# Layer 1's third pair of down weights placed behind x's rooms, and four norm steps beside each first product of the MLA

## Chip, cores and metric

One core of a Trainium2 chip runs the whole kernel in one launch. The metric is the device time of that launch in microseconds (us). Five engines work side by side, each through its own queue in order: TensorE (PE, matmuls; PEld is its loading of stationary operands), VectorE (DVE), ScalarE (ACT), GpSimd (POOL) and SyncE (SP), which here only issues transfers (DMA).

## The reference

Two layers over 1024 latent tokens (`lat`) and 256 context tokens (`cx`) of width 1024, all in float32. Layer 0 mixes with a gated MLP and a gated DeltaNet, layer 1 with multi-head latent attention (MLA); each layer ends in a convolutional feed-forward network (FFN), and a final norm follows. Cut to what matters here:

```
def conv_ffn(h, w_up, conv_w, w_down):
    g, u = jnp.split(dwconv(h @ w_up, conv_w), 2, axis=-1)      # 2 x 2816 columns
    return (jax.nn.silu(g) * u) @ w_down
...
def mla_mixer(h_ctx, h_lat, w_in, ...):
    z_lat = h_lat @ w_in          # 384 query, 256 key/value, 64 rotary columns
    ...
for i in range(2):
    h_lat = modulate(rms_norm(lat, norm1_g[i]), sh1, sc1)       # the same for the context
    lat = lat + g1 * mixer(h_lat)
    lat = lat + g2 * conv_ffn(modulate(rms_norm(lat, norm2_g[i]), sh2, sc2), w_up, conv_w, w_down)
return rms_norm(lat, final_g)
```

## The kernel before

Activations lie transposed: 128 features on the partitions, tokens along the row. Every float32 product is made of three matmuls on halves: an operand is split into a high half (`...h`, rounded) and a low half (`...l`, the rest), and hh, hl and lh are summed in PSUM. A weight tile of 128x1024 is loaded by a DMA (`wdr`, `wur`: raw), its high half is made on POOL (line 126) and its low half on DVE (line 133).

The instructions are recorded in the order of the Python code, where generators advance side work in steps; a scheduler then sets the final order of each engine's queue from a timeline that it simulates when the kernel is built, under the dependences between tiles. On the chip each engine keeps that order.

**FFN.** `ffn_up` makes the 22 gated rows (`y1`) one after the other: products into PSUM, copies into `raw0` and `raw1`, the convolution into `y0` and `y1`, the gate (line 427) and a store to DRAM (`act<-y`, line 428). These four rows of 4 KB a partition lie in the pool `ffc1` (layer 1). `ffn_down` then takes chunks of tokens (in layer 0 512, 256, 256, 256; in layer 1 512, 256, 256). A chunk has two halves of four output tiles, a half has 11 steps, a step is one weight tile and 24 matmuls (lines 633 to 635, output `dn`). The activations come back from DRAM in groups (`al<-act`, line 571; split into `ah` on ACT and `al` on DVE). The first two weight tiles are prepared inside `ffn_up`'s last round. Which room a pair of halves gets is told by its number i:

```
p, bufs = (wp, 2) if i % 3 < 2 else (self.ffz, 1)
W[i] = [p.tile([P, KD, P], F32R, tag="wu" + a, name="wd" + a, bufs=bufs) for a in "hl"]
```

So pairs 2, 5, 8, ... use the pool `ffz1`. I call the pairs of layer 1's down product W0, W1, W2, ...: W0 is `wdh_26813`, W1 `wdh_26857`, W2 `wdh_26889` (from `wdr_26861`), W3 `wdh_26928`, W4 `wdh_26965`, W5 `wdh_26995`, W6 `wdh_27032`, W7 `wdh_27062`. The pool `ffx1` holds the residual chunks (`x`), which are loaded from DRAM and to which a half's products are added (line 650) at its end. Pools are allocated one behind the other: `ffz1` was allocated first, at the address where `ffc1` lay (bytes 85568 to 93760 of a partition, which were `raw0` and `raw1` of the up stage), then `ffx1` (93760 to 118336).

**The norm at the end of layer 0.** When a chunk of layer 0's down product is done, `tail0` norms and modulates it into `h` for layer 1 (`mod_h`): squares on ACT and POOL, four matmuls of 32 rows each for two sums (`nsum`, line 196), a copy on DVE (line 214), one matmul (`nall`, line 217), a chain over DVE and ACT (lines 219 to 230), then the modulated halves `h1h`, `h1l`, `h2h`, `h2l`. With `steps` it is a generator of ten steps. For the last chunk (256 tokens, `x_15250`) four of them run beside the down product, and `self.pend` holds the other six: four with squares (the first of these four issues the first `nsum`), one with the second `nsum` and its copy, and one with `nall` and all the rest. `mla_early` makes the MLA's first products (`proj`, lines 140 to 142): two weight tiles t for three chunks c of 512, 256 and 256 tokens. `mla_in` then makes those two products for the last chunk, which need its `h`, and goes on with norms of keys (`nsum<-nsq`) and the queries' products.

Of the kernel before, what the change touches and what calls it, by code (L numbers as in the profile page):

```python
# [61 lines left out]
def drain(*gens):  # L62
    for g in gens:
        for _ in g:
            pass
# [32 lines left out]
class Kern:  # L98
# [445 lines left out]
    def ffn_down(self, l, wp, chunks, groups, tile_x, x, g2, tail, early=None):  # L544
# [59 lines left out]
        def run():  # L604
# [49 lines left out]
            self.pend = pend  # L654
        self.X = X
        return run()

    def tail_rooms(self, pool):
# [835 lines left out]
    def mla_early(self, get, hv, pend):  # L1494

        ps = {}
        for t in range(KVT):
            for c in range(3):
                ps[t, c] = self.proj(get(t), hv, None, *CHB[c])
                next(pend, None)  # L1500
            get(t + 1)
        drain(pend)
        return ps
# [328 lines left out]
    def run(self):  # L1832
        nc, tc, I = self.nc, self.tc, self.I
        with ExitStack() as es:
# [208 lines left out]
            xp = []  # L2043
# [75 lines left out]
            def tail1(i):  # L2119
# [4 lines left out]
                for k in range(KD):  # L2124
# [7 lines left out]
                    if k % 2:  # L2132
# [4 lines left out]
            down = self.ffn_down(1, ffw, END, groups, None, load_x(END), lambda c0: g2[:, 0], tail1)  # L2137
            self.ffn_up(1, ffw, SEQ, (0, lambda t: t.rearrange("p (s c) -> p s c", c=256)[:, 2:4, :]), [(0, SEQ, 0)], None,
                        (begin0, begin1, begin2), late, down)
            self.ffz = tc.alloc_tile_pool(name="ffz1", bufs=1)  # L2140
            xp.append(tc.alloc_tile_pool(name="ffx1", bufs=1))
            tp = tc.alloc_tile_pool(name="fft1", bufs=1)
            tmp1 = self.tail_rooms(tp)
            drain(down)
            drain(self.pend)
            tp.release()
            xp[0].release()
            self.ffz.release()
            hcl.release()
            hce.release()  # L2150
            ffw.release()
# [82 lines left out]
```

## Time and profile before

| | |
|---|---|
| median of 3 runs | 3269.45 us (3264.09 to 3271.99) |
| the profiled execution | 3260.52 us, of which the span from first to last instruction 3258.5 us |
| PE busy | 3104.7 us, 95% of the span |
| DVE, POOL, ACT busy | 2165.1, 1306.6, 1103.8 us |
| PE's longest wait | 13.16 us, at 2982 to 2995 us of the span |

Times in rows are microseconds from the start of the span, durations of groups are means in ns. A row of a timeline has start, duration, engine, line, operation, output and inputs, shapes and count, and in brackets how long the engine had idled before and what released it. The releaser is inferred from semaphores. Matmuls overlap: one of 256 columns is shown with 0.28 us, but the next starts 0.12 us later, so rates are read from starts.

### The profile page before, as it was taken

Reading aid. Unit: us, or ns where it says so; the run is one execution under the profiler, and the core shown is the slowest. Engines: PE = TensorE matmul, PEld = TensorE weight load, DVE = VectorE, ACT = ScalarE, POOL = GpSimd, SP = SyncE. Lnnn points to the kernel's source line nnn. Section 1 sums busy time; section 2 is a strip of 40 time slices with the busy share of each in tenths; the row PEclk is TensorE's granted clock in tenths of the full one; section 3 lists DMA queues with packets and bytes.
Section 4 is the critical chain, followed back from the end, with each engine's and each line's share of the span. In section 5 each row is a group of like instructions: output and inputs, shape, how many; then the busy total and the mean of one; then the engine's idle time right before and its main releaser. Section 6 shows DMA issues by size and latency. Waiting matters only on the chain. (4 is left out here: it accounts for less than half of the span.)

```text
span 3258.5 us, 48694 instructions
## 1 busy us (share of the span) xinstructions
PE 3104.7 (95%) x19029; PEld 2596.4 (80%) x19029; DVE 2165.1 (66%) x3218; ACT 1103.8 (34%) x2136; POOL 1306.6 (40%) x1181
## 2 busy tenths in 40 slices
PE   7999899998999999999999999999999899998998
PEld 5667777896777788888899778988978787776888
DVE  6333877566876578874577456666667888887365
ACT  5322233333432233340111255555533333333110
POOL 4234323553443354532455132122134566663243
PEclk9999999999999999999999999999999999999999
DMA  7344957753144522145467131000033122225464
GB/s 253 123 143 126 302 142 217 223 168 117 40 147 147 160 96 70 64 154 173 143 225 223 54 115 38 27 22 22 8 121 119 51 79 81 82 82 207 141 196 150
DMA packets 254436, 411.40 MB, mean 126 GB/s; under 512 B 46576, under 2 KB 163520, under 8 KB 254080
## 3 DMA queue, kind: packets, MB, share of 16 engines
q1 hardware_dynamic: 254208, 408.31, 39.1%
q8 instruction: 150, 2.46, 0.3%
q14 instruction: 78, 0.64, 0.1%
HBM read 327.47 MB, written 80.78 MB: 125 GB/s over the span
## 5 line engine op out<-in xcount | busy, mean ns | idle before, releaser
L633 PE MATMUL dn<-ah,wdh 128*128 128x256 f32 (+1 forms) x1232 | 388.9, 317 | 15.8 <-POOL wdh L126 13.7
L635 PE MATMUL dn<-ah,wdl 128*128 128x256 f32 (+1 forms) x1232 | 383.8, 318 | 14.5 <-DVE wdl L133 14.5
L634 PE MATMUL dn<-al,wdh 128*128 128x256 f32 (+1 forms) x1232 | 386.7, 315 | 0.0
L126 POOL TENSOR_SCALAR wdh<-wdr 128x1024 fp32r<-128x1024 f32 x154 | 194.5, 1264 | 361.6 <-PE dn L634 232.5
L133 DVE TENSOR_TENSOR wdl<-wdr,wdh 128x1024 fp32r<-128x1024 f32 x154 | 200.2, 1304 | 198.1 <-POOL wdh L126 194.2
L633 PEld LDWEIGHTS dn<-ah,wdh 128*128 128x128 f32 x1232 | 235.4, 191 | 38.1 <-POOL wdh L126 14.7
L635 PEld LDWEIGHTS dn<-ah,wdl 128*128 128x128 f32 x1232 | 233.1, 191 | 33.8 <-DVE wdl L133 17.3
L634 PEld LDWEIGHTS dn<-al,wdh 128*128 128x128 f32 x1232 | 235.2, 191 | 15.3
L126 POOL TENSOR_SCALAR wuh<-wur 128x1024 fp32r<-128x1024 f32 x106 | 138.8, 1310 | 215.6 <-PE upc L409 112.1
L133 DVE TENSOR_TENSOR wul<-wur,wuh 128x1024 fp32r<-128x1024 f32 x106 | 164.2, 1549 | 90.9 <-POOL wuh L126 90.9
L1720 POOL TENSOR_SCALAR p<-p,rsm 128x1280 f32<-128x1280 f32 x63 | 84.6, 1343 | 325.9 <-DVE rsm L1713 176.9
L675 DVE SCALAR_TENSOR_TENSOR y<-raw,fconv,y 128x1023 f32<-128x1023 f32 (+1 forms) x132 | 175.0, 1354 | 31.8 <-ACT y L420 31.4
L140 PE MATMUL proj<-hh,wih 128*128 128x512 f32 (+1 forms) x512 | 183.9, 361 | 0.0
L677 DVE SCALAR_TENSOR_TENSOR y<-raw,fconv,y 128x1023 f32<-128x1023 f32 (+1 forms) x132 | 182.9, 1407 | 0.1
L142 PE MATMUL proj<-hh,wil 128*128 128x512 f32 (+1 forms) x512 | 177.2, 347 | 1.1 <-DVE wil L133 1.1
L141 PE MATMUL proj<-hl,wih 128*128 128x512 f32 (+1 forms) x512 | 177.7, 348 | 0.0
L427 POOL TENSOR_TENSOR y<-y,y 128x1280 f32<-128x1280 f32 (+1 forms) x42 | 119.8, 2852 | 108.1 <-issue 58.0
L393 POOL TENSOR_TENSOR s<-wur 128x512 f32<-128x512 f32 x42 | 70.2, 1671 | 183.2 <-DMA wur<-in_w_up 142.2
L1702 DVE TENSOR_REDUCE mx<-sc 128x1 f32<-128x512 f32 (+1 forms) x192 | 114.5, 596 | 40.2 <-PE sc L1701 38.1
L420 ACT ACTIVATE y<-raw,fconv 128x1280 f32<-128x1280 f32 (+1 forms) x88 | 110.6, 1259 | 81.1 <-DVE raw L436 74.7
L111 ACT ACTIVATE p<-sc,nmx 128x512 f32<-128x512 f32 (+1 forms) x192 | 116.0, 617 | 49.3 <-DVE nmx L1706 49.1
L140 PEld LDWEIGHTS proj<-hh,wih 128*128 128x128 f32 x512 | 98.3, 193 | 20.2 <-issue 7.7
(544 smaller groups left out, 9290.3 us busy)
## 6 DMA issues: line engine op xcount, KB each, us to landing
wdr<-in_w_down SPq DMA_DIRECT2D x154, 512.0 KB, 3.8
adaw<-in_ada_w SPq DMA_DIRECT2D x96, 512.0 KB, 4.2
wur<-in_w_up SPq DMA_DIRECT2D x88, 512.0 KB, 3.6
al<-act SPq DMA_DIRECT2D x20, 1024.0 KB, 7.7
t<-t SPq DMA_DIRECT2D x20, 768.0 KB, 6.4
act<-y SPq DMA_DIRECT2D x22, 640.0 KB, 2.9
act<-y SPq DMA_DIRECT2D x22, 512.0 KB, 2.6
wir<-in_w_t SPq DMA_DIRECT2D x20, 512.0 KB, 4.5
```

Of the source, the lines that this page charges most:

```text
L111: self.nc.scalar.activation(out, in_, func, **kw)
L126: nc.gpsimd.tensor_scalar(dst, src, 1.0, 0.0, op0=ALU.mult, op1=ALU.add)
L133: (self.nc.gpsimd if eng == "pools" else self.nc.vector).tensor_tensor(lo, src, f(hi), ALU.subtract)
L140: nc.tensor.matmul(ps, wh, xh, start=first and i == 0, stop=False)
L141: nc.tensor.matmul(ps, wh, xl, start=False, stop=False)
L142: nc.tensor.matmul(ps, wl, xh, start=False, stop=last and i == n - 1)
L427: (nc.gpsimd if ci < FT - 1 else nc.vector).tensor_tensor(y[1], y[0], y[1], ALU.mult)
L633: nc.tensor.matmul(pss[o], wh[:, q, :], ah, start=pr == j == 0, stop=False)
L634: nc.tensor.matmul(pss[o], wh[:, q, :], al, start=False, stop=False)
L635: nc.tensor.matmul(pss[o], wl[:, q, :], ah, start=False, stop=pr == npr - 1 and j == 1)
L675: nc.vector.scalar_tensor_tensor(out=y[:, s0 + 1:e], in0=raw[:, s0:e - 1], scalar=w[:, 0:1], in1=y[:, s0 + 1:e], op0=ALU.mult, op1=ALU.add)
L677: nc.vector.scalar_tensor_tensor(out=y[:, s0:e - 1], in0=raw[:, s0 + 1:e], scalar=w[:, 2:3], in1=y[:, s0:e - 1], op0=ALU.mult, op1=ALU.add)
```

## The change

Two edits. In `mla_early` each product is followed by four steps of the pending norm instead of one, so that the six steps stand behind the first two of the six products instead of one behind each. In layer 1 `ffx1` is allocated before `ffz1`: x's rooms now lie at 85568 to 110144 and W2's room at 110144 to 118336, behind them; the two releases change places too.

```
@@ mla_early
             for c in range(3):
                 ps[t, c] = self.proj(get(t), hv, None, *CHB[c])
-                next(pend, None)
+                for _ in range(4):
+                    next(pend, None)
             get(t + 1)
@@ run, layer 1
+            xp.append(tc.alloc_tile_pool(name="ffx1", bufs=1))
             self.ffz = tc.alloc_tile_pool(name="ffz1", bufs=1)
-            xp.append(tc.alloc_tile_pool(name="ffx1", bufs=1))
             tp = tc.alloc_tile_pool(name="fft1", bufs=1)
...
             tp.release()
+            self.ffz.release()
             xp[0].release()
-            self.ffz.release()
```

PE in `mla_early`, behind the first weight tile's product for the context chunk (`h0`), as a piece of the difference; `t_12979` to `t_12982` are the squares, `t_12983` the copied sums:

```order
 L141 MATMUL proj<-h0l,wuh 128x256
 L142 MATMUL proj<-h0h,wul 128x256
+L196 MATMUL nsum<-t_12980,cst_66 32x256
+L196 MATMUL nsum<-t_12981,cst_66 32x256
+L196 MATMUL nsum<-t_12982,cst_66 32x256
+L196 MATMUL nsum<-t_12979,cst_66 32x256
+L217 MATMUL nall<-t_12983,cst_66 128x256
 L140 MATMUL proj<-h1h,wuh 128x256
 L141 MATMUL proj<-h1l,wuh 128x256
```

The second `nsum` and `nall` moved 72 and about 100 matmul rows ahead, and now follow each other with nothing between; before, `nsum` stood behind the second weight tile's product for the context chunk, and `nall` behind the last product, right ahead of the one that needs the result. ACT, DVE and POOL keep their order around the norm up to its end. On DVE the copy of the sums stands, before and now, behind two low halves of the MLA's query weights:

```order
L133 TENSOR_TENSOR wql_16602<-wqr_16599,wqh_16601 128x384
L133 TENSOR_TENSOR wql_16778<-wqr_16775,wqh_16777 128x384
L214 COPY t4_12983<-nsum_15749 128x256
L219 TENSOR_SCALAR t0_12979<-nall_16047 128x256
L229 SCALAR_TENSOR_TENSOR t1_12980<-t1_12980,t0_12979 128x256
```

Only the number of `nall`'s bank differs in these rows from before.

POOL at the passage from layer 1's up to its down product (`y1_26614` is the gate of the 21st row). Before:

```order
L427 TENSOR_TENSOR y1_26614<-y0_26613,y1_26614 128x1024
L126 TENSOR_SCALAR wdh_26813<-wdr_26811 128x1024
L126 TENSOR_SCALAR wdh_26857<-wdr_26817 128x1024
L126 TENSOR_SCALAR wdh_26928<-wdr_26893 128x1024
L126 TENSOR_SCALAR wdh_26965<-wdr_26932 128x1024
L126 TENSOR_SCALAR wdh_26889<-wdr_26861 128x1024
L126 TENSOR_SCALAR wdh_26995<-wdr_26969 128x1024
```

and now:

```order
L427 TENSOR_TENSOR y1_26614<-y0_26613,y1_26614 128x1024
L126 TENSOR_SCALAR wdh_26889<-wdr_26861 128x1024
L126 TENSOR_SCALAR wdh_26813<-wdr_26811 128x1024
L126 TENSOR_SCALAR wdh_26857<-wdr_26817 128x1024
L126 TENSOR_SCALAR wdh_26928<-wdr_26893 128x1024
L126 TENSOR_SCALAR wdh_26965<-wdr_26932 128x1024
L126 TENSOR_SCALAR wdh_26995<-wdr_26969 128x1024
```

W2's high half moved from behind W4 to ahead of W0; its low half moved on DVE in the same way, from behind the last row's gate to ahead of W0's low half. PE's sequence of steps (0, 1, 2, ...) is the same. SP at the same passage (`y1_26754` is the 22nd row, `al_27097` the activations of rows 18 to 21 for the first chunk). Before:

```order
L571 DMA al_27030<-act_82 128x4x512
L557 DMA wdr_26893<-in_w_down 128x1024
L571 DMA al_27322<-act_82 128x8x256
L557 DMA wdr_26932<-in_w_down 128x1024
L557 DMA wdr_26969<-in_w_down 128x1024
L557 DMA wdr_26999<-in_w_down 128x1024
L428 DMA act_82<-y1_26754 128x1024
L2049 DMA x_26895<-xs_81 128x8x512
L571 DMA al_27097<-act_82 128x4x512
```

and now:

```order
L557 DMA wdr_26893<-in_w_down 128x1024
L571 DMA al_27030<-act_82 128x4x512
L557 DMA wdr_26932<-in_w_down 128x1024
L571 DMA al_27322<-act_82 128x8x256
L557 DMA wdr_26969<-in_w_down 128x1024
L557 DMA wdr_26999<-in_w_down 128x1024
L557 DMA wdr_27036<-in_w_down 128x1024
L428 DMA act_82<-y1_26754 128x1024
L557 DMA wdr_27066<-in_w_down 128x1024
L2050 DMA x_26895<-xs_81 128x8x512
L571 DMA al_27097<-act_82 128x4x512
```

The raw weights of W3 moved ahead of one load of activations, those of W4 ahead of another, and W7's ahead of the last row's store, with W8's behind it.

More of the change, by code (lines that the diff above doesn't have):

```diff
@@ L1499, in mla_early @@
                 ps[t, c] = self.proj(get(t), hv, None, *CHB[c])
-                next(pend, None)
+                for _ in range(4):
+                    next(pend, None)
             get(t + 1)
@@ L2139, in run @@
                         (begin0, begin1, begin2), late, down)
+            xp.append(tc.alloc_tile_pool(name="ffx1", bufs=1))
             self.ffz = tc.alloc_tile_pool(name="ffz1", bufs=1)
-            xp.append(tc.alloc_tile_pool(name="ffx1", bufs=1))
             tp = tc.alloc_tile_pool(name="fft1", bufs=1)
@@ L2146, in run @@
             tp.release()
+            self.ffz.release()
             xp[0].release()
-            self.ffz.release()
             hcl.release()
```

## The prediction

> **What bounds the kernel now.** I read the page's busy times first, then PE's waits along the whole span, then the two places of the change stage by stage, and last the timelines of the engines on which PE waits there. The page:
>
> ```profile
> span 3258.5 us, 48694 instructions
> PE 3104.7 (95%) x19029; PEld 2596.4 (80%) x19029; DVE 2165.1 (66%) x3218; ACT 1103.8 (34%) x2136; POOL 1306.6 (40%) x1181
> PE   7999899998999999999999999999999899998998
> ```
>
> PE works nearly everywhere, so only PE's time counts: its waits, and the stretches in which it is slow. No instruction is taken away by the change, so what can be won is what PE loses at the two places.
>
> Place 2, the start of layer 1's down product, has the longest wait of the kernel. Busy time by stage (PE, PEld, DVE, ACT, POOL; then granted clock, DMA share, GB/s), and PE's and POOL's timelines:
>
> ```profile
> 2971.20:2976.80 5.60, 5.60 (x26) 4.50 (x25) 5.05 (x6) 5.26 (x6) 1.06 (x1) 1.00 1.06 373
> 2982.40:2995.50 13.10, 0.00 (x0) 0.00 (x0) 8.23 (x9) 1.06 (x1) 2.33 (x2) 0.70 0.34 120
> 2995.50:3003.80 8.30, 8.25 (x25) 6.53 (x26) 1.23 (x1) 0.00 (x0) 0.00 (x1) 0.65 0.99 346
> 3003.80:3009.40 5.60, 5.60 (x25) 4.51 (x24) 3.59 (x3) 2.01 (x2) 1.05 (x1) 1.00 1.07 375
> ```
> ```profile
> 2982.01 0.39 PE L635 MATMUL dn<-ah,wdl 128*128 128x512 f32 x1
> 2995.55 0.79 PE L633 MATMUL dn<-ah,wdh 128*128 128x512 f32 x1 [13.16 <-POOL wdh L126]
> ```
> ```profile
> 2959.65 2.41 POOL L427 TENSOR_TENSOR y<-y,y 128x1024 f32<-128x1024 f32 x1 [6.75 <-DVE y L677]
> 2965.67 1.60 POOL L126 TENSOR_SCALAR wdh<-wdr 128x1024 fp32r<-128x1024 f32 x1 [3.61 <-PE upa L409]
> 2971.24 1.06 POOL L126 TENSOR_SCALAR wdh<-wdr 128x1024 fp32r<-128x1024 f32 x1 [3.97 <-issue]
> 2982.26 1.43 POOL L126 TENSOR_SCALAR wdh<-wdr 128x1024 fp32r<-128x1024 f32 x1 [4.01 <-PE dn L634]
> 2994.46 1.04 POOL L126 TENSOR_SCALAR wdh<-wdr 128x1024 fp32r<-128x1024 f32 x1 [10.77 <-DMA act<-y]
> ```
>
> A step takes 5.6 us; steps 0 and 1 end at 2982.4. Then PE stands until W2's high half comes, and by the order of POOL that is the split at 2994.46, which was held by the store of the last up row, because the old room of W2 lay on `ffc1`. The 13.1 us without a matmul are followed by a stretch at a granted clock of 0.65, in which step 2 takes 8.3 us.
>
> Place 1 is the end of `mla_early`:
>
> ```profile
> 1802.64 0.28 PE L140 MATMUL proj<-h1h,wuh 128*128 128x256 f32 x1
> 1813.95 0.64 PE L196 MATMUL nsum<-t,cst 128*32 128x256 f32 x8
> 1814.52 0.38 PE L140 MATMUL proj<-h1h,wuh 128*128 128x256 f32 x1
> 1817.49 0.59 PE L217 MATMUL nall<-t,cst 128*128 128x256 f32 x2
> 1822.00 0.58 PE L140 MATMUL proj<-h1h,wuh 128*128 128x256 f32 x1 [3.91 <-ACT h1h L253]
> 1833.32 1.05 PE L196 MATMUL nsum<-nsq,cst 128*32 128x512 f32 x4
> ```
> ```profile
> 1822.00:1826.00 4.00, 3.58 (x12) 2.80 (x12) 3.89 (x8) 2.35 (x5) 1.98 (x3) 0.50 0.00 0
> 1826.00:1830.00 4.00, 3.21 (x13) 2.63 (x13) 1.89 (x5) 2.34 (x7) 1.36 (x2) 0.50 0.00 0
> ```
>
> `nall` at 1817.49 is the last thing PE can do without the last chunk's `h`; it waits 3.91 us for the first `h1h`, then runs at clock 0.50, with small waits for each next `h`, up to 1830. The 48 matmuls of the last chunk's two products fill 1818 to 1833; at the rate of the row pair 1814.52 and 1817.49 (24 matmuls in 2.97 us) they would take 5.9.
>
> **The change part by part.** *Place 2.* W2 now lies where `xa2` was, which `late` had released long before, so POOL waits only for the raw weights. By the new order W2's split stands right behind the gate at 2959.65, which ends at 2962.06, and ahead of W0's, which begins at 2965.67 because PE frees its room then. The gap of 3.61 us takes 1.1 to 1.6 us of split. The low half on DVE (1.2 us like the others) falls among DVE's rows of 2961 to 2967:
>
> ```profile
> 2961.62 2.65 DVE L133 TENSOR_TENSOR al<-al,ah 128x1024 fp32r<-128x1024 f32 x2 [0.59 <-ACT ah L124]
> 2964.20 0.68 DVE L436 TENSOR_TENSOR raw<-upe,raw 128x512 f32<-128x512 f32 x1
> 2967.31 1.23 DVE L133 TENSOR_TENSOR wdl<-wdr,wdh 128x1024 fp32r<-128x1024 f32 x1 [0.95 <-POOL wdh L126]
> ```
>
> The 0.95 us of idle ahead of W0's low half take most of it; what is left (0.3 us) delays nothing, since step 0 begins only when the up products end at 2971.2. So the edit costs nothing there, covered by those gaps. Step 2 then follows step 1 at 2982.4 and ends at 2988.0 instead of 3003.8: a gain of 15.8 us, 13.1 of wait and 2.7 of slow clock.
>
> What is late next? W3 and W4 are needed at 2988.0 and 2993.6; their raw loads go out earlier than before, and their splits do not wait for W2 any more. W4's high half is the split at 2982.26, and its low half was done before the last gate on DVE, which ended at 2990.6, as the store of that row shows, which goes out at once:
>
> ```profile
> 2990.66 0.33 SPq L428 DMA_DIRECT2D act<-y  x1
> 2994.36 0.58 SPq L2049 DMA_DIRECT2D x<-xs  x1
> 2995.00 0.65 SPq L571 DMA_DIRECT2D al<-act  x1
> 3005.35 2.01 ACT L124 ACTIVATE ah<-al 128x1024 fp32r<-128x1024 f32 x2 [21.42 <-DMA al<-act]
> ```
>
> So W4 is ready at least 3 us ahead of its step. W5 takes W2's room when step 2 ends (2988.0), and is needed at 2999.2. The last activations (`al_27097`) are ready after ACT's 2.0 us from 3005.35 and one more low half of 1.2, at 3009; steps 9 and 10 use them, and step 9 now begins at 2982.4 + 7 x 5.6 = 3021.6. Slack 12 us. On SP the store now stands behind W7's raw load too, which waits for W4's low half; that one is ahead of the gate on DVE anyhow, so the store goes out as before. x's rooms still cover `y1`, as they did; x is first needed after step 10. From there on all follows PE's steps, so I take the whole 15.8.
>
> *Place 1.* `nsum` comes at 1802.64, where the last square is ready (below, POOL, 1801.52 plus 0.61), and takes 0.57 (1813.95 to 1814.52). `nall` follows at once, but needs the copy on DVE, and that stands behind the second `wql`, which waits for a transfer:
>
> ```profile
> 1801.52 0.61 POOL L206 TENSOR_TENSOR t<-x 128x256 f32<-128x256 f32 x1
> 1804.13 0.52 POOL L126 TENSOR_SCALAR wqh<-wqr 128x384 fp32r<-128x384 f32 x1 [2.00 <-DMA wqr<-in_w_uq]
> 1804.68 0.56 DVE L133 TENSOR_TENSOR wql<-wqr,wqh 128x384 fp32r<-128x384 f32 x1 [2.13 <-POOL wqh L126]
> 1814.73 0.42 DVE L214 COPY t<-nsum 128x256 f32<-128x256 f32 x1 [9.49 <-PE nsum L196]
> 1828.79 0.48 DVE L254 SCALAR_TENSOR_TENSOR h2l<-t,mv,h2h 128x256 fp32r<-128x256 f32 x1 [0.58 <-ACT h2h L253]
> ```
>
> The copy runs from 1805.24 to 1805.66, `nall` at about 1805.8: a new wait of PE of 2.6 us (1803.2 to 1805.8), with everything on PE queued behind it, and no other engine waiting for that. Then the 96 matmuls between 1802.64 and 1817.49, less `nsum`, take 14.85 - 0.57 = 14.3 us, to 1820.3 with `nall`'s own 0.24. The norm's chain took 11.8 us from `nall` to the last `h2l` (1817.49 to 1829.27); from 1805.8 it ends at 1817.6, so the last `h` is ready 2.7 us before PE asks for it. The 48 matmuls end at 1826.2. `nsum<-nsq`, at 1833.32 before, needs key rows that ACT copies right behind the norm, so from 1817.6; it can follow. Gain: 33.3 - 26.2 = 7.1 us.
>
> Unknown is whether the new 2.6 us wait brings a slow stretch. Rows after waits of nearly that length go both ways:
>
> ```profile
> 1466.95 0.50 PE L635 MATMUL dn<-ah,wdl 128*128 128x512 f32 x1 [2.80 <-DVE wdl L133]
> 1648.62 0.39 PE L635 MATMUL dn<-ah,wdl 128*128 128x256 f32 x1 [2.75 <-DVE wdl L133]
> 1649.93 0.41 PE L633 MATMUL dn<-ah,wdh 128*128 128x256 f32 x1
> 1652.92 0.32 PE L634 MATMUL dn<-al,wdh 128*128 128x256 f32 x1
> ```
>
> After 1466.95 the rate is the usual one. After 1648.62 it is usual for a microsecond, then from 1649.93 to 1652.92 the matmuls are shown with 0.41 instead of 0.28 us, 14 in 3.0 us, where 0.12 us each would make 1.7: a loss of 1.3 to 1.6 us. So 0 to 1.6; I take the middle, 0.8. Less than nothing it can't be.
>
> [...]
>
> The sum: 15.8 + 7.1 - 0.8 = 22.1 us. Against the profiled execution (3260.52 us) that gives 3238.4; that execution was faster than the three runs (lowest 3264.09), so against their median, 3269.45, it gives 3247.3.
>
> **The rivals.** *The new PE wait costs more* (10 in 100). If PE stays slow after 1805.8 as it did from 1822 to 1830, 8 us at half rate, that costs 4 us more than no stretch; then place 1 gives 3 and the time is 3269.45 - 18.8 = 3250.7. For it: the clock of 0.50 in two rows above; against it: those followed a longer wait and were full of small ones.
>
> *Place 2 gets a new wait in place of the old one* (13 in 100). W2 is now at the head of POOL's queue, with W0 and W1 behind it. DMA is full here (share 1.06), and if W2's raw weights landed at 2968 rather than before 2965, W0's two halves would be ready at 2968 + 1.1 + 1.6 + 1.2 = 2972, 0.8 us late; each further microsecond costs one. Or W3's or W4's low half is late because the activations ahead of it on DVE came behind two weight loads (0.5 MB each at 373 GB/s, 2.8 us together), against slacks of about 3 us. Price 4 to 8 us: 3251 to 3255.
>
> *It does little* (4 in 100): W2's split is held by something else in the same place, and only place 1 gives its 7: 3262, within 0.3%.
>
> *Slower* (3 in 100). The last row's store, x and `al_27097` wait in SP's queue behind W7's raw load, which waits for W4's low half. If DMA were backed up there, step 9 would wait for `al_27097`: from 3021.6 on each microsecond is lost, and after 23 us, from 3045 on, the kernel is slower than before; landing at 3055, 46 us later than worked out above, it would give 3280. Against it: DMA share in 2982 to 2995 is 0.34.
>
> **How the numbers follow.** The forecast has 70 in 100 and gives 3247. A measurement of this kernel can tell about 0.3%, 10 us, from no change. Forecast, both first rivals: faster (93 in 100); little: same (4); slower 3. The range: down to 3237, if the runs lie as near to the profiled execution as they may (9 us) and no clock is lost, and up to 3256, the second rival's upper end.
>
> **What would show it.** Right: PE has no wait between steps 1 and 2, step 2 takes 5.6 us at clock 1.00, POOL makes W2 before W0; at place 1 PE waits about 2.6 us at `nall` for DVE, and no more for `h1h`; from `nsum` to `nsum<-nsq` PE needs about 23.6 us instead of 30.7. Wrong, if PE waits again at steps 2 to 4 or 9 of place 2, if `nall`'s wait grows with a later `wqr`, or if a later stage, such as the attention's first weights, gives back what PE won.

## The result, and the profile after

The changed kernel takes 3246.2 us (median of four runs, 3243.5 to 3249.4) against 3267.8 us for the kernel before, timed beside it (four runs, 3264.1 to 3272.0): a ratio of 0.9935, with a 95% interval of 0.9923 to 0.9947, so 21.6 us less. Its profiled execution took 3249.41 us (span 3247.3), the slowest of its four; that of the kernel before, 3260.52, was the fastest of its own. The two profiles therefore differ by only 11.2 us, and a reader who subtracts the two spans gets half of the result. What follows compares stretch with stretch instead.

The page after, the lines that answer to those shown of before:

```profile
span 3247.3 us, 48696 instructions
PE 3106.5 (96%) x19029; PEld 2599.4 (80%) x19029; DVE 2167.6 (67%) x3218; ACT 1105.0 (34%) x2136; POOL 1305.6 (40%) x1181
PE   7999899998999999999999999999999899999998
```

PE's busy time is nearly what it was (3104.7 before), so by the two pages the span shrank by idle time. Stretches at a low clock count as busy, though (in the kernel before, 8.25 of the 8.30 us from 2995.50 on, at a granted clock of 0.65), so what those cost can't be read here.

Place 2 after: four stretches of 5.60 us, about the length of a step, in layer 1's down product, the first three within steps 0 to 3, the last in steps 8 and 9 (columns as before: PE, PEld, DVE, ACT, POOL, granted clock, DMA share, GB/s), and POOL at the passage:

```profile
2970.20:2975.80 5.60, 5.60 (x25) 4.51 (x24) 5.50 (x7) 4.09 (x4) 1.34 (x1) 1.00 1.05 383
2977.60:2983.20 5.60, 5.60 (x26) 4.63 (x25) 5.60 (x5) 2.99 (x6) 1.76 (x1) 1.00 0.22 84
2983.20:2988.80 5.60, 5.60 (x26) 4.57 (x25) 5.60 (x7) 0.67 (x1) 1.30 (x1) 1.00 0.34 94
3016.80:3022.40 5.60, 5.60 (x26) 4.58 (x25) 1.39 (x2) 0.00 (x0) 1.05 (x1) 1.00 0.31 102
```
```profile
2958.67 2.41 POOL L427 TENSOR_TENSOR y<-y,y 128x1024 f32<-128x1024 f32 x1 [6.75 <-DVE y L677]
2961.86 1.22 POOL L126 TENSOR_SCALAR wdh<-wdr 128x1024 fp32r<-128x1024 f32 x1 [0.78 <-PE upe L409]
2964.69 1.51 POOL L126 TENSOR_SCALAR wdh<-wdr 128x1024 fp32r<-128x1024 f32 x1 [1.61 <-PE upa L409]
2970.27 1.34 POOL L126 TENSOR_SCALAR wdh<-wdr 128x1024 fp32r<-128x1024 f32 x1 [4.07 <-issue]
```

W2 is split at 2961.86, W0 behind it at 2964.69, W1 at 2970.27: the gap behind the last gate holds W2's split, and W0 is no later than it was against its step. PE is busy for all of 5.60 us at a clock of 1.00 in each of these stretches, and its timeline has no wait from the first `dn` at 2970.19 to the end of chunk 0 at 3092.2.

Place 1 after, rows of PE, then of DVE, then the stretches behind `nall`:

```profile
1804.23 0.64 PE L196 MATMUL nsum<-t,cst 128*32 128x256 f32 x8
1807.57 1.22 PE L217 MATMUL nall<-t,cst 128*128 128x256 f32 x2 [2.69 <-DVE t L214]
1829.39 1.05 PE L196 MATMUL nsum<-nsq,cst 128*32 128x512 f32 x4
```
```profile
1806.62 0.56 DVE L133 TENSOR_TENSOR wql<-wqr,wqh 128x384 fp32r<-128x384 f32 x1 [2.22 <-POOL wqh L126]
1807.10 0.42 DVE L214 COPY t<-nsum 128x256 f32<-128x256 f32 x1
```
```profile
1808.00:1810.00 2.00, 2.00 (x9) 1.82 (x9) 0.42 (x1) 0.61 (x2) 0.00 (x0) 0.50 0.32 98
1810.00:1812.00 2.00, 2.00 (x17) 2.00 (x16) 1.23 (x3) 0.64 (x2) 0.26 (x1) 0.86 0.00 0
```

There is no wait for `h1h` any more, and a wait of 2.69 us at `nall`, as forecast: the copy starts at 1807.10, right behind the second `wql` of 1806.62. But behind it the clock is 0.50 for most of three microseconds.

To set the stretches side by side I took, from PE's timeline of each profiled execution, the starts of the same rows, and their differences in us. A: from the first `nsum` of the last chunk's norm (its first four squares) to `nsum<-nsq`. B: layer 1's up products, first `upa` to first `dn`. C: chunk 0 of the down product, first `dn` to the last matmul of 512 columns. D: from there to the wait of 3.0 us for `wdl`, which lies within chunk 1. The last column is the difference of the medians, kernel less the kernel before as it was timed beside it; the kernels from e1 on are told below.

| kernel | first `nsum` at | A | B | C | D | against before |
|---|---|---|---|---|---|---|
| before | 1799.1 | 34.2 | 467.7 | 138.1 | 39.1 | |
| changed | 1800.6 | 28.8 | 471.7 | 122.0 | 43.3 | -21.6 |
| changed again | 1804.0 | 28.6 | 472.5 | 122.0 | 39.1 | -22.9 |
| changed, third time | 1801.9 | 28.7 | 469.2 | 122.0 | 39.1 | -25.3 (one run) |
| e1: steps alone | 1798.2 | 27.0 | 468.3 | 139.0 | 39.1 | -8.1 |
| e2: rooms alone | 1808.4 | 34.2 | 469.4 | 122.0 | 39.1 | -15.5 |
| e3: two steps | 1801.6 | 25.4 | 469.0 | 122.0 | 40.5 | -28.0 |
| e4: four raw rooms | 1800.5 | 28.6 | 457.7 | 122.0 | 39.1 | -33.2 |
| e5: pad | 1804.0 | 35.6 | 469.1 | 122.0 | 39.1 | -14.6 |
| e6: e3 and e4 | 1805.7 | 25.4 | 458.3 | 122.0 | 39.1 | -33.2 |
| e7: copy on ACT | 1801.5 | 25.3 | 468.7 | 122.0 | 39.1 | -25.9 |
| e8: e7 and e4 | 1802.9 | 25.6 | 458.3 | 122.0 | 39.1 | -36.0 |

The first column is a warning: no edit touches the stages ahead of it, and yet it spreads from 1798.2 to 1808.4. The difference of two spans tells nothing below 10 us; the stretch C is the same to 0.1 us in all ten executions with the room moved.

### The profile page after: what moved, and what is told of

It is laid out like the page before. It is cut to its first block, busy times and chain, and to the rows that moved or that the text cites. A ratio compares the mean times of both kernels' runs of the same rounds, so it can differ in the third digit from the quotient of the medians.

```text
span 3247.3 us, 48696 instructions
## 1 busy us (share of the span) xinstructions
PE 3106.5 (96%) x19029; PEld 2599.4 (80%) x19029; DVE 2167.6 (67%) x3218; ACT 1105.0 (34%) x2136; POOL 1305.6 (40%) x1181
## 5 line engine op out<-in xcount | busy, mean ns | idle before, releaser
L124 ACT ACTIVATE ah<-al 128x512 fp32r<-128x512 f32 (+1 forms) x77 | 52.4, 744 | 185.2 <-DMA al<-act 174.9
```

## The experiments

**The two parts alone (e1, e2).** e1 is the kernel before with the four steps and the pools in their old order; e2 has the pools swapped and one step:

```
e1:  -                next(pend, None)
     +                for _ in range(4):
     +                    next(pend, None)
e2:  +            xp.append(tc.alloc_tile_pool(name="ffx1", bufs=1))
                  self.ffz = tc.alloc_tile_pool(name="ffz1", bufs=1)
     -            xp.append(tc.alloc_tile_pool(name="ffx1", bufs=1))
```

> Only the four steps per product; layer 1's rooms stay in the old order. If place 1's gain is kept, as the profile after the change has it (25.2 us from `nsum` to `nsum<-nsq` instead of 30.7), it is 5.5 to 6.5 us faster than before, with a PE wait of about 2.7 us at `nall` and the 13.1 us wait at W2 still there. If the attention gives it back, 0 to 2 us. [...]

> Only the order of the two pools; one step per product as before. The step from 1 to 2 of layer 1's down product is worth 15.8 us by the sum. If the loss at the passage from chunk 0 to chunk 1 (wait of 2.39 us for DVE and 4 to 6 us in all in the profile after) follows from the earlier start, this kernel has it too and is 10 to 12 us faster than before; if that loss was chance of one execution, it is 15 to 17 us faster and its profile has no PE wait over 1 us at the end of chunk 0.

e1 took 3261.13 us against 3269.19 for before (ratio 0.9975, 0.9965 to 0.9986), e2 3253.73 (0.9953, 0.9939 to 0.9966). The parts add up: 8.1 and 15.5 make 23.5, against 21.6 and 22.9 in the two timings of both. e1 keeps the hole of place 2, as its row shows:

```profile
1804.66 0.70 PE L217 MATMUL nall<-t,cst 128*128 128x256 f32 x2 [2.23 <-DVE t L214]
1825.13 1.05 PE L196 MATMUL nsum<-nsq,cst 128*32 128x512 f32 x4
2989.00 0.79 PE L633 MATMUL dn<-ah,wdh 128*128 128x512 f32 x1 [13.84 <-POOL wdh L126]
```

e1's execution also shows what place 1 gives without a slow stretch: behind a wait of 2.23 us its clock stayed at 1.00 (the first four microseconds from the start of `nall`),

```profile
1804.66:1806.66 2.00, 2.00 (x15) 1.95 (x16) 0.42 (x1) 0.70 (x2) 0.00 (x0) 1.00 0.35 98
1806.66:1808.66 2.00, 2.00 (x17) 1.91 (x16) 1.31 (x4) 0.55 (x2) 0.35 (x1) 1.00 0.00 0
```

and A is 27.0, 7.2 us less than before (the forecast's 7.1). That is more than the 5.5 to 6.5 us of the expectation's first case, which was reckoned from the changed kernel's profile, with the slow stretch in it. The 8.1 us of its time, with an interval of 4.6 to 11.4 us, exclude only that the attention gives the gain back. e2 has no wait over 1 us at the end of chunk 0, and D is 39.1.

**Where the first profile of the changed kernel lost more (two repeats).** That profile had 4.2 us more than before in D. There DVE came late to chunk 0's evictions (L650); PE's row, then DVE's:

```profile
3097.11 0.38 PE L633 MATMUL dn<-ah,wdh 128*128 128x256 f32 x1 [2.39 <-DVE x L650]
```
```profile
3093.06 2.20 DVE L133 TENSOR_TENSOR al<-al,ah 128x512 fp32r<-128x512 f32 x3 [6.83 <-ACT ah L124]
3095.18 1.21 DVE L133 TENSOR_TENSOR wdl<-wdr,wdh 128x1024 fp32r<-128x1024 f32 x1
3096.32 2.71 DVE L650 SCALAR_TENSOR_TENSOR x<-dn,mv,x 128x512 f32<-128x512 f32 x4
```

I suspected a loop that the earlier start had made too tight: the activations' load on SP waits behind weight loads, these for a raw room that a `wdl` on DVE frees, and that `wdl` stands behind the low halves of the load before. The rival was chance.

> The changed kernel once more, for a second profile. The first one lost, beside the kernels with one part of the change, 4 us in the up stage of layer 1 (a wait of 3.77 instead of 2.15 us for DVE at the second group and what follows it), 4.2 us between the end of chunk 0 and the wait at the start of chunk 2's products, and 1.6 us behind that. If these were chance of that execution, this one shows 468 us, 39.1 us and 99.7 us for the three stretches and a time of 3240 to 3246 us; if they belong to the change, 471 to 472, 43 and 101 us again.

> The changed kernel a third time, one look. Same two readings as for the run before it. Place 1: if a wait of 2.3 to 2.7 us at `nall` is at the edge of a clock drop, some executions show clock 0.50 behind it and some 1.00, with 28.6 to 28.8 us against about 27 from the first `nsum` to `nsum<-nsq`.

The first repeat took 3244.45 us (ratio 0.9922, 0.9906 to 0.9938), the second, a single execution, 3242.0. (The wait at "chunk 2's products" in the expectation lies within chunk 1.) In both D is 39.1. The repeat's rows of DVE, to set beside those of the first profile:

```profile
3093.07 1.90 DVE L133 TENSOR_TENSOR al<-al,ah 128x512 fp32r<-128x512 f32 x3 [4.35 <-ACT ah L124]
3094.88 1.22 DVE L133 TENSOR_TENSOR wdl<-wdr,wdh 128x1024 fp32r<-128x1024 f32 x1
3096.02 2.72 DVE L650 SCALAR_TENSOR_TENSOR x<-dn,mv,x 128x512 f32<-128x512 f32 x4
```

Chunk 0's last matmul starts at 3092.2 in the first profile and at 3097.4 in the repeat (first `dn` plus C). Against it DVE's evictions begin 4.1 us late in the one and 1.4 us ahead in the other, with the same code, and the wait of DVE for ACT's `ah` is 6.83 and 4.35 us. Of the ten executions with the room moved D was long in one, a little long (40.5) in e3, and usual in the other eight. So the loss varies from execution to execution and is not a regular cost of the change; with only two executions in the old order (both 39.1), whether the earlier start makes it likelier is not shown, nor why ACT's `ah` came late. B was long (471.7 and 472.5) in two of three and 469.2 in the third, where e1 to e3, e5 and e7 have 468.3 to 469.4, so about 3 us at most. Part of it is a wait of PE for `raw` some 87 us into the up stage: 3.74 to 3.77 us in all three executions and 3.72 in e3, but 2.14 to 2.16 in before, e1, e2, e5 and e7. Since e7 has both parts of the change, whether the change has part in it stays open.

**Whether the room or the order of the pools made the hole (e5).** The kernel before, with 16 KB a partition of nothing ahead of the extra weights:

```
+            pad = tc.alloc_tile_pool(name="pad1", bufs=1)
+            pad.tile([P, 4096], F32, name="pad")
             self.ffz = tc.alloc_tile_pool(name="ffz1", bufs=1)
             xp.append(tc.alloc_tile_pool(name="ffx1", bufs=1))
```

> The kernel before, with an unused pool of 16 KB ahead of the extra weights' pool; the two pools stay in the old order and the steps at one per product. The extra weights' room then lies behind the rooms of `ffc1`, and x's further back. If the lying on `ffc1`'s rows made W2 late, the hole of 13 us between steps 1 and 2 is gone and the time is that of the two pools swapped, 15 to 16 us less than before (3252 to 3256 us). If the order in which the pools are taken did it, the hole stays and the time is that of before. x's loads are earlier here than in the changed kernel; if x waiting for `y1`'s store cost anything there, this one is faster than the swap by that.

It took 3252.77 us (0.9946, 0.9932 to 0.9960), like e2. (Its A is 1.4 us longer than that of before; no run here shows why.) POOL at place 2, PE in step 2, and SP:

```profile
2970.55 1.44 POOL L126 TENSOR_SCALAR wdh<-wdr 128x1024 fp32r<-128x1024 f32 x1 [0.56 <-DMA wdr<-in_w_down]
2973.59 1.52 POOL L126 TENSOR_SCALAR wdh<-wdr 128x1024 fp32r<-128x1024 f32 x1 [1.60 <-PE upa L409]
```
```profile
2990.20:2995.80 5.60, 5.60 (x26) 4.65 (x25) 5.60 (x5) 0.85 (x1) 1.75 (x1) 1.00 1.09 358
```
```profile
2977.78 3.13 SPq L2049 DMA_DIRECT2D x<-xs  x2
3002.79 0.39 SPq L571 DMA_DIRECT2D al<-act  x1
```

The order of the pools is the old one and the hole is gone: it was W2's room lying in the place of `ffc1`. Moved off it, W2 goes ahead of W0 in POOL's queue of itself. (In e5 x's rooms are off `ffc1` too, in e2 they are on it; the hole is gone in both.)

One thing the prediction does not say: the wait went by the whole pool, not by the rows under the room. W2's room lay on `raw0` and `raw1`, while the store that ended its wait reads `y1`, another row of `ffc1`. The last reader of `raw0` and `raw1` is the convolution on DVE, in the kernel before:

```profile
2984.68 1.27 DVE L677 SCALAR_TENSOR_TENSOR y<-raw,fconv,y 128x1023 f32<-128x1023 f32 x1
```

It ends at 2985.95, and W2's split starts 8.5 us later, at 2994.46, when the store of `y1` is through. So what the new room waited for is the last use of the pool that was there before it.

x's loads go out at 2977.8 in e5, far ahead of the last row's store (2996.5), and that gains nothing against e2 (14.6 and 15.5): x was not late. The last activations' load is no earlier to speak of: it goes out 23.7 us behind the first `dn` in e5 (2979.1 by PE's timeline) and 25.3 in the changed kernel (2970.2 to 2995.5).

**Two steps instead of four (e3).** `range(2)` in place of `range(4)` in `mla_early`.

> After the change, but two steps of the norm per product instead of four. `nsum` and `nall` then come a product or more later, and the copy on DVE no longer stands behind the late second `wql`. If the 2.7 us wait and the half-clock stretch behind it are the price of taking four steps, the wait shrinks below 1 us, the clock stays at 1.00 and the kernel is 2 to 4 us faster than the changed one (19 to 26 us less than before). If the chain of the norm then ends too late (last `h2l` after PE asks for it), part of the old wait for `h1h` comes back and it is 0 to 3 us slower than the changed one.

3241.18 us (0.9916, 0.9902 to 0.9930). PE, and DVE, at place 1:

```profile
1809.41 0.70 PE L217 MATMUL nall<-t,cst 128*128 128x256 f32 x2 [0.63 <-DVE t L214]
1827.03 1.05 PE L196 MATMUL nsum<-nsq,cst 128*32 128x512 f32 x4
```
```profile
1807.18 0.56 DVE L133 TENSOR_TENSOR wql<-wqr,wqh 128x384 fp32r<-128x384 f32 x1 [2.13 <-POOL wqh L126]
1808.93 0.42 DVE L214 COPY t<-nsum 128x256 f32<-128x256 f32 x1 [1.19 <-PE nsum L196]
```

The late `wql` is past when `nsum` comes; the copy waits for `nsum` alone, PE for 0.63 us, and there is no slow stretch: the granted clock is 1.00 from 1808 to 1812. A is 25.4, 8.8 us less than before and 3.3 less than the changed kernel's mean of three (28.7). By the medians e3 is 5.0 and 3.3 us faster than the two timings of the changed kernel, and 28.0 us faster than before, more than the 19 to 26 expected; the intervals overlap, so it is A that carries this.

**The copy on another engine (e7).** With e3 the wait could also have gone because the whole chain came later. So four steps again, but the copy within `mla_early` on ACT:

```
-        nc.vector.tensor_copy(part[:32 * g, :cn], ps[:32 * g, :cn])
+        (nc.scalar.copy if self.ca else nc.vector.tensor_copy)(part[:32 * g, :cn], ps[:32 * g, :cn])
```

> The changed kernel, four steps per product, but within `mla_early` ACT instead of DVE copies the norm's sums out of PSUM. ACT has nothing to do between the last square and the logarithm. If `nall` waits because the copy stands on DVE behind the second `wql`, whose transfer is late, the wait of 2.3 to 2.7 us shrinks to 0.6 to 0.8 us (the copy itself), the clock stays at 1.00, and the stretch from the first `nsum` to `nsum<-nsq` takes 25 to 25.5 us as with two steps per product, instead of 28.6 to 28.8: 3 to 3.5 us faster than the changed kernel. If the early `nsum` itself (the squares) sets the end of the wait, it stays over 2 us and the time is that of the changed kernel.

3241.83 us (0.9926, 0.9910 to 0.9941). Its lines stand one further down than in the others:

```profile
1806.38 0.70 PE L218 MATMUL nall<-t,cst 128*128 128x256 f32 x2 [0.57 <-ACT t L215]
```
```profile
1807.57 0.56 DVE L134 TENSOR_TENSOR wql<-wqr,wqh 128x384 fp32r<-128x384 f32 x1 [2.04 <-POOL wqh L127]
1808.05 0.42 DVE L220 TENSOR_SCALAR t<-nall 128x256 f32<-128x256 f32 x1
```

The wait is 0.57 us and A is 25.3; the interval overlaps those of the changed kernel, so here too A carries the reading. So the copy's place in DVE's queue, behind a `wql` that waited for a transfer, is the cause of the 2.7 us. In the changed kernel the copy starts 0.48 us behind the `wql`'s start (1806.62 and 1807.10), though the sums were there some 2.2 us before it (`nsum`, 1804.23 plus 0.64). In e7 the `wql` still holds the next step of the norm (the reading of `nall`, at 1808.05), but PE has matmuls meanwhile.

**Four rooms for the raw weights (e4), and the best of both (e6, e8).** For the loop that I suspected, `bufs=4` instead of 3 for layer 1's raw weights (four lines: up, down, and two in the output projection):

```
-                raws[i] = wp.tile([P, KD, P], F32, tag="wur", name="wdr", bufs=3)
+                raws[i] = wp.tile([P, KD, P], F32, tag="wur", name="wdr", bufs=3 + l)
```

> After the change, but four rooms instead of three for layer 1's raw weights, so that SP can issue the activations' loads one weight load earlier. If the loop of SP, the load of the activations, ACT's high halves, DVE's low halves and back to SP (period 12.0 to 14.5 us where two steps of PE take 11.2) makes DVE late at the end of chunk 0, the wait of 2.39 us there goes and the kernel is 3 to 6 us faster than the changed one. If DVE's work alone, or chance, makes it late, the wait stays or goes without a change of the median by more than 2 us.

3235.95 us (0.9905, 0.9891 to 0.9918), more than I expected, and not where I expected it. C and D are what they are without it; B is 457.7 instead of 468 to 472. Two steps of the up stage on SP, three rooms (the changed kernel) and then four, and how often and how long PE waited at L408 for DVE's `raw` in that stage (us, times); each time the changed kernel's third execution first, then e4:

```profile
2710.07 12.05 SPq L382 DMA_DIRECT2D wur<-in_w_up  x2
2730.03 11.89 SPq L382 DMA_DIRECT2D wur<-in_w_up  x2
```
```profile
2710.26 7.17 SPq L382 DMA_DIRECT2D wur<-in_w_up  x2
2729.65 7.18 SPq L382 DMA_DIRECT2D wur<-in_w_up  x2
```
```profile
  DVE raw L436: 10.5, 15
```
```profile
  DVE raw L436: 0.6, 1
```

The period is 19.96 us with three rooms and 19.39 with four, and the waits for `raw` at that line fall from 10.5 us to 0.6. A pair of loads is issued within 7.2 us instead of 12; that this earlier issue is what lets DVE keep up was not tried by itself. It answers nothing on D, which the repeats settled. It does show place 1 once more: a wait of 2.36 us at `nall`, and a clock of 0.50:

```profile
1807.13 0.70 PE L217 MATMUL nall<-t,cst 128*128 128x256 f32 x2 [2.36 <-DVE t L214]
```
```profile
1808.00:1810.00 2.00, 2.00 (x11) 2.00 (x10) 0.62 (x2) 1.25 (x3) 0.00 (x0) 0.50 0.23 78
```

> The changed kernel with two steps per product and four rooms for layer 1's raw weights. Four rooms gained 10 us, and by the profile in the up stage of layer 1 (457.7 instead of 468 us; the waits of 0.37 us for `raw` at every step are gone), not in the down product; two steps gained 3.4 us by the profile at place 1 (25.4 instead of 28.8 us). If both stand, the time is 3230 to 3234 us, 35 to 39 us less than before. If the up stage takes back what place 1 wins, 3235 to 3238 us.

> The same with four rooms for layer 1's raw weights: a candidate that should beat both kernels. By the sum of the stretches 10 us from the up stage and 3.3 us from place 1 on top of the changed kernel: 3229 to 3233 us, no slower than the version with two steps per product and four rooms (3234.2 us).

e6 took 3234.19 us (0.9891, 0.9876 to 0.9905), e8 3231.73 (0.9889, 0.9875 to 0.9902): 33.2 and 36.0 us less than before. e8 came out as expected. e6 did not: it missed the 35 to 39 us, and against the kernel before it is no faster than e4 (33.2 too). Each has both gains in its stretches (A 25.4 and 25.6, B 458.3), but e6's profiled execution reached the first `nsum` 5.2 us later than e4's, so 3 us more or less at place 1 can't be seen in its time. The intervals do not tell e4, e6 and e8 apart.

## Why the prediction was right, point by point

*Place 2, 15.8 us: right, 16.1 by C.* The wait (13.1) and the slow clock behind it (2.7) were one hole, and nothing took its place. e5 shows the cause to be the one named, W2's room on `ffc1`; that the whole pool counts, and not the rows beneath, the prediction left open.

*Its cover: right.* W2 in the 3.6 us gap behind the gate cost nothing, W3, W4 and W5 were in time (no wait of PE in chunk 0, clock 1.00), and so were x and the last activations:

```profile
2990.86 0.33 SPq L428 DMA_DIRECT2D act<-y  x1
2994.89 0.58 SPq L2050 DMA_DIRECT2D x<-xs  x1
2995.53 0.65 SPq L571 DMA_DIRECT2D al<-act  x1
```
```profile
3007.03 2.01 ACT L124 ACTIVATE ah<-al 128x1024 fp32r<-128x1024 f32 x2 [23.16 <-DMA al<-act]
```

The store goes out at 2990.86 (2990.66 before) and ACT splits the last activations at 3007.0; step 9 begins near 3020 in this execution (2970.19 plus nine steps of 122.0/22 us). So the rivals "a new wait in place of the old one", "it does little" and "slower" did not come about.

*Place 1, 7.1 us less 0.8 for the clock: the first right, the second too small.* Without a slow stretch e1 gave 7.2. The wait at `nall` was 2.2 to 2.7 us (2.6 forecast), and the last `h` was in time. But the slow stretch came in four of the five executions with four steps and the copy on DVE. Those four take 28.7 us in A, e1 takes 27.0. Of these 1.7 us, 0.3 lie ahead of `nall`, in longer waits, and 1.4 behind it (21.8 to 22.0 us from `nall` to `nsum<-nsq`, 20.5 in e1), which is what the slow clock cost: near the upper bound (0 to 1.6), not the middle. The step that was off is the choice of 0.8 between rows that pointed both ways. From the second `nsum` to `nsum<-nsq` PE therefore took 25.2 us in the first profile (1804.23 to 1829.39), not 23.6.

*The rival "the new PE wait costs more": in part.* The slow stretch was there, but lasted about 3 us, not 8. There are no small waits for `h` in it, as there were in the old one; that the clock came back sooner for that reason was not tried.

*"A later stage gives back": not as a rule.* The loss of 4.2 us in D was there in one execution of the changed kernel and absent in the other two.

*The sum: 22.1 forecast.* By the stretches 16.1 + 5.5 = 21.6; by the medians 21.6 and 22.9. The reckoning from the median of before rather than from its fast profiled execution was needed: 3260.52 - 22.1 would have been 3238.4, against 3246.2 measured. That 3247.3 came within 1.1 us is partly luck: the kernel before, timed again beside the changed one, had a median 1.6 us lower than the one reckoned from, and the two stretches missed by 0.3 and 0.8 us in opposite directions.

## What to carry to other kernels

When an engine waits for a weight long after it was loaded, look at what lay at the place of the room it is split into: a room in the place of a pool that a late store still reads waited for that store, even where the store reads other rows of the pool (here until 8.5 us after the last use of the rows beneath it), and either another order of the pools or an unused pad moved it off. When work is pulled forward so that a matmul needs a small step of another engine, see what stands ahead of that step in that engine's queue: here a copy behind a split that waited for a transfer cost the tensor engine a wait of 2.2 to 2.7 us. Fewer steps at a time, or the copy on an idle engine, was worth 3.3 us of stretch A here. Set stretches of several executions side by side before you explain a difference of spans: here two spans of the same work differed by 10 us before the change even began.

## What the runs showed of the hardware

At `nall`, waits of PE of 2.33, 2.36, 2.67 and 2.69 us were each followed by about 3 us at a granted clock of 0.50, and waits of 2.23, 0.63 and 0.57 by none (clock 1.00 behind them in e1, e3 and e7). Length alone does not tell the two apart: in the kernel before, the wait of 2.80 us ahead of 1466.95 has a clock of 1.00 behind it for at least 6 us, while behind the 2.75 us ahead of 1648.62 it is 0.98 over the first microsecond and 0.50 from 1649.93 to 1652.93. What else decides is not shown by these runs. Where the drop falls differs: in the third execution of the changed kernel, after 2.67 us, the clock is down when PE starts again; in the first repeat, after 2.33 us, it drops later (the repeat's `nall` and stretches first, then the third execution's stretches, each from the start of `nall`):

```profile
1810.62 0.70 PE L217 MATMUL nall<-t,cst 128*128 128x256 f32 x2 [2.33 <-DVE t L214]
```
```profile
1810.62:1812.60 1.98, 1.98 (x11) 1.93 (x12) 0.42 (x1) 0.69 (x2) 0.00 (x0) 0.74 0.38 99
1812.60:1814.60 2.00, 2.00 (x11) 2.00 (x11) 1.30 (x4) 0.57 (x2) 0.34 (x1) 0.50 0.00 0
```
```profile
1808.89:1810.89 2.00, 2.00 (x7) 1.82 (x8) 0.42 (x1) 0.21 (x1) 0.00 (x0) 0.50 0.36 98
1810.89:1812.89 2.00, 2.00 (x15) 2.00 (x14) 0.83 (x2) 1.04 (x3) 0.00 (x0) 0.77 0.00 0
```

A mean of 0.74 over 1.98 us is about a microsecond at 1.00 and one at 0.50, if the clock had no other value there (an estimate from the 1.00 and 0.50 of the other stretches): there PE had work again before the clock fell.
